# First chunk: q of all heads over its h blocks, k and v beside the h of the next chunks, weights from ScalarE's queue

## The chip, the cores and the metric

The kernel runs on one core of one Trainium2 chip. The metric is the device time of one execution in microseconds; the number compared is the median of several runs. The engines of the core are TensorE (PE; its weight loads are PEld), VectorE (DVE), ScalarE (ACT), GpSimd (POOL) and SyncE (SP), which issues most of the DMAs.

## The reference, cut to what matters

One layer over 2048 tokens of width 1024, in float32:

```
mod = silu(c) @ W_ada + b_ada                  # shift, scale, gate
h = rms_norm(x, norm_g) * (1 + scale) + shift
u = h @ W_in                                   # GLU input, gate_a, q, k, v, gate_b, m_a, m_b
q, k = head_rms_norm(q, q_gain), head_rms_norm(k, k_gain)    # 8 heads of 64
y_a = swish(layer_norm(conv31(glu))) * silu(gate_a) @ W_conv_out
o = stick_breaking_attention(q, k, v)
y_b = (o * silu(gate_b)) @ W_sb_out
x = x + gate * ((sigmoid(m_a) * y_a + sigmoid(m_b) * y_b) @ W_out)
```

## The kernel before, in words

Every matrix product is made of three fp32r products: each operand is split into a high part (a cast) and a low part (operand minus high part), and hi·hi, hi·lo and lo·hi are added in PSUM (`mm3`, `nat_mm`). The tokens are in four chunks of 512, worked from the last to the first (`ORDER`); h of a chunk is held transposed, as eight blocks `kc` of 128 features by 512 tokens, each with a high and a low tile.

**Weights.** `split_into` loads a piece of 128 x 1024 in two halves through two buffers `wl` (SP's queue), casts the half on ScalarE (L109) and subtracts it on GpSimd (L110). A group of q, k or v (256 columns, four heads) is two pieces. Groups 0 and 1 are q, 2 and 3 k, 4 and 5 v.

**The first chunk (pool `hx`).** x tiles are loaded, squared on ScalarE and scaled by the reciprocal root of the mean square (`xn_pair`): three Newton steps, for the first two tiles on VectorE, for the other two on GpSimd. Then a loop over the eight h blocks: two columns of W_ada are loaded and reduced against silu(c) on VectorE (`mod_col`, L225), the one-column scale a_s and shift b_s are made on VectorE (L408, L410), four transposes of x on TensorE give the block, ScalarE makes hf = a_s * x + b_s and its cast hhi, GpSimd the low part hlo (VectorE in the last block). TensorE adds the block's part of q of heads 0 to 3 (group 0), in two PSUM tiles; q of heads 4 to 7 (group 1) is a second loop over the blocks.

**The next chunks.** `h_half` makes h of two x tiles at a time for the chunks ORDER[1], ORDER[2] and, in pool `hz` once `hx` is closed, ORDER[3]: ScalarE hf, VectorE the cast hhi (L366), GpSimd or VectorE hlo (L367). `qk_group` normalises q or k per head: small squares on ScalarE (L272), `head_norm` on VectorE (the root, and qn, L287), `transposed` (four transposes, qhi on ScalarE, qlo on VectorE, L307, one buffer each, four stores to DRAM on SP's queue). For the first chunk's q its squares and `head_norm` run in this part; its transposes run later, through pool `cvp`.

**The rest of the first stage.** With q group 0 of the other chunks done, the stage goes over glu, gate, q, k and v groups in a written order, with matmuls kept in program order on TensorE (`pin`). Each tile ends in a `tick`, which emits RATE taps of the depthwise convolution on VectorE (L485) from a list. PSUM has five buffers `pd`. Here k's two groups and v's first run over all four chunks, v's second (`v_group`) in the next stage, beside the LayerNorm, whose generator `ln` takes a step per tile. Then come the attention and the output stage.

A scheduler orders the instructions of each engine by priority, in the order of the program unless told otherwise; each engine then issues in that fixed order.

Of the kernel before, what the change touches and what calls it, by code (L numbers as in the profile page):

```python
# [8 lines left out]
F32 = mybir.dt.float32  # L9
# [9 lines left out]
P = 128  # L19
# [13 lines left out]
NXT = 7  # L33
NWA = 4
RATE = 2.6
# [15 lines left out]
def trunk_kernel(  # L51
# [29 lines left out]
    def rsqrt(pool, v, n, tag, pool_eng=False, keep=lambda i: i):  # L81
# [3 lines left out]
        keep((nc.gpsimd if pool_eng else nc.vector).tensor_scalar(  # L85
            out=y.bitcast(I32), in0=v.bitcast(I32), scalar1=-0.5, scalar2=MAGIC,
            op0=ALU.mult, op1=ALU.add))
        for _ in range(3):
            if pool_eng:
                nc.gpsimd.tensor_tensor(out=t, in0=y, in1=y, op=ALU.mult)  # L90
                nc.gpsimd.tensor_tensor(out=t, in0=t, in1=v, op=ALU.mult)
                nc.gpsimd.tensor_scalar(out=t, in0=t, scalar1=-0.5, scalar2=1.5,
                                        op0=ALU.mult, op1=ALU.add)
                nc.gpsimd.tensor_tensor(out=y, in0=t, in1=y, op=ALU.mult)
            else:
                keep(nc.vector.scalar_tensor_tensor(out=t, in0=y, scalar=-0.5, in1=y,
                                                    op0=ALU.mult, op1=ALU.mult))
                keep(nc.vector.tensor_tensor(out=t, in0=t, in1=v, op=ALU.mult))
                keep(nc.vector.scalar_tensor_tensor(out=y, in0=t, scalar=1.5, in1=y,
                                                    op0=ALU.add, op1=ALU.mult))  # L100
# [12 lines left out]
    def load_piece(pool, src):  # L113
        hi = pool.tile([P, 1024], F32R, tag="whi", name="whi")
        lo = pool.tile([P, 1024], F32R, tag="wlo", name="wlo")
        split_into(src, hi, lo)
        return hi, lo
# [64 lines left out]
    with ExitStack() as s1:  # L182
# [39 lines left out]
        def mod_col(j, ca, wa):  # L222

            nc.sync.dma_start(wa, w_ada[j])
            nc.vector.scalar_tensor_tensor(out=wa, in0=wa, scalar=1.0, in1=ca,  # L225
                                           op0=ALU.mult, op1=ALU.mult,
                                           accum_out=mod[:, j:j + 1])
# [29 lines left out]
        def qk_group(grp, isk, chunks=ORDER, w2=None, ps0=None):  # L257

            w2 = w2 or ps0 or [piece(w_qkv[grp, i]) for i in range(2)]
            h4 = (grp % 2) * 4  # L260
            dst = kst_d if isk else qst_d
            for b in chunks:
                ssq = sm.tile([P, 4, 4], F32, tag="ssq", name="ssq")
                qn = qp.tile([P, 4, 4, HD], F32, tag="qn", name="qn", bufs=2)
                pss = []
                for half in range(2):
                    ps = ps0[half] if ps0 else nat_tile(pd, w2, b, half)
# [25 lines left out]
        def transposed(qn, pr, dst, h4, b, isk):  # L293
# [5 lines left out]
            hi = cvp.tile([P, CH], F32R, tag="qhi", name="qhi", bufs=1)  # L299
            lo = cvp.tile([P, CH], F32R, tag="qlo", name="qlo", bufs=1)  # L300
# [23 lines left out]


# [3 lines left out]
        def xn_pair(tb0, pool, bufs, pool_eng=False):  # L329
            ss = sm.tile([P, 2], F32, tag="ss", name="ss")  # L330
# [7 lines left out]
            nc.vector.tensor_scalar(out=ss, in0=ss, scalar1=1.0 / D, scalar2=EPS,  # L338
                                    op0=ALU.mult, op1=ALU.add)
            r = rsqrt(sm, ss, 2, "nx", pool_eng)  # L340
            for i in range(2):
                nc.vector.tensor_scalar(out=xs[i], in0=xs[i], scalar1=r[:, i:i + 1],
                                        scalar2=None, op0=ALU.mult)
# [25 lines left out]
        def h_half(g, o, pool, bufs, on_dve):  # L369
            xs = xn_pair(4 * g + o, pool, bufs)  # L370
# [5 lines left out]
        with tc.tile_pool(name="hx", reuse_waits="tile", bufs=1) as hx:  # L376
            g0 = ORDER[0]
            w2_q1 = [(hx.tile([P, D], F32R, name=f"w1h{i}"), hx.tile([P, D], F32R, name=f"w1l{i}"))
                     for i in range(2)]
# [5 lines left out]
            xs = xn_pair(4 * g0, hx, NXT)  # L385
            for o in range(0, D, CH):
# [5 lines left out]
            xs += xn_pair(4 * g0 + 2, hx, NXT, True)  # L392
            ba = load_const(b_ada, 24, "ba")
            ng = load_const(norm_g, KC, "ng")
            ba1 = sm.tile([P, KC], F32, name="ba1", bufs=1)
            nc.vector.tensor_scalar(out=ba1, in0=ba[:, KC:2 * KC], scalar1=1.0, scalar2=None,
                                    op0=ALU.add)
            w2_q0 = []
            qk_ps = [[pd.tile([P, 2, 256], F32, tag="pd", name="pd") for _ in range(2)]
                     for _ in range(2)]  # L400
            for kc in range(KC):
                for j in (8 + kc, kc):
                    mod_col(j, ca, hx.tile([P, D], F32, tag="wa", name="wa", bufs=NWA))
                if kc < 2:
                    w2_q0.append(load_piece(wpa, w_qkv[0, kc]))
                elif kc in (4, 5):
                    split_into(w_qkv[1, kc - 4], *w2_q1[kc - 4])
                nc.vector.tensor_tensor(out=b_s[:, kc:kc + 1], in0=mod[:, kc:kc + 1],  # L408
                                        in1=ba[:, kc:kc + 1], op=ALU.add)
                nc.vector.scalar_tensor_tensor(out=a_s[:, kc:kc + 1], in0=mod[:, 8 + kc:9 + kc],  # L410
                                               scalar=ba1[:, kc:kc + 1], in1=ng[:, kc:kc + 1],
                                               op0=ALU.add, op1=ALU.mult)
                modulate(x_block(xs, kc), hx.tile([P, CH], F32, tag="hf", name="hf", bufs=6),
                         g0, 0, kc, (1, 1),
                         nc.gpsimd if kc < KC - 1 else nc.vector)
                for half in range(2):
                    for i in range(2):
                        nat_mm(qk_ps[0][half], w2_q0, g0, half, i, kc,
                               kc == 0 and i == 0, kc == KC - 1 and i == 1)
            for kc in range(KC):  # L420
                for half in range(2):
                    for i in range(2):
                        nat_mm(qk_ps[1][half], w2_q1, g0, half, i, kc,
                               kc == 0 and i == 0, kc == KC - 1 and i == 1)
            for o in (0, 2):
                h_half(ORDER[1], o, hx, NXT, ())
            qk_group(0, False, ORDER[:1], ps0=qk_ps[0])
            for o in (0, 2):
                h_half(ORDER[2], o, hx, NXT, (0, 4))
            qk_group(1, False, ORDER[:1], ps0=qk_ps[1])  # L430
# [3 lines left out]
        with tc.tile_pool(name="hz", reuse_waits="tile", bufs=1) as hz:  # L434
# [6 lines left out]
            gain = load_const(q_gain, 1, "gain")  # L441
            gk = load_const(k_gain, 1, "gk")
            nc.vector.tensor_tensor(out=gain, in0=gain, in1=gk, op=ALU.mult)


        with tc.tile_pool(name="cvp", reuse_waits="tile", bufs=2, side="right") as cvp:
# [101 lines left out]
            def v_block(grp):  # L548
                w2 = [piece(w_qkv[grp, i]) for i in range(2)]
                h4 = (grp % 2) * 4  # L550
                for b in ORDER:
# [19 lines left out]
            qk_group(2, True)  # L571
            v_block(4)
            glu(3)
            qk_group(3, True)
# [10 lines left out]
        with ExitStack() as sl:  # L585
# [110 lines left out]
            def v_group(grp):  # L696
                w2 = [piece(w_qkv[grp, i]) for i in range(2)]
                h4 = (grp % 2) * 4
                for b in ORDER:
# [397 lines left out]
```

## Time and profile before

| | us |
|---|---|
| median of 3 runs | 1903.24 (1902.55 to 1905.62) |
| profiled execution | 1899.99 |
| its span | 1898.2 |
| TensorE busy in it | 1805.2 (95%) |
| VectorE, ScalarE, GpSimd busy | 1230.8, 807.6, 693.8 |

The rows further down are of the one profiled execution. A busy TensorE is not TensorE at its peak: a matmul of the same size takes longer at the lower of its clocks, and matmuls overlap, so the distance between two starts tells the rate. "Idle before" names what an engine waited for.

### The profile page before, as it was taken

How to read it: one execution, taken by the hardware profiler on the slowest of the kernel's cores; microseconds unless marked ns; L12 is line 12 of the kernel's file. 1: busy time of each engine (PE TensorE's matmuls, PEld its weight loads, DVE VectorE, ACT ScalarE, POOL GpSimd, SP SyncE). 2: the span in 40 equal slices, each digit the busy share in tenths (PEclk: the TensorE clock that was granted, in tenths of full speed). 3: DMA queues.
4: the chain of work that ended last, by engine and by line, in shares of the span. 5: the costliest groups of instructions: out<-in, count | busy, mean ns of one | idle time of the engine just before them, and what ended most of it. 6: DMA issues, size and time to landing. Idle time of an engine off the chain costs nothing.

```text
span 1898.2 us, 27437 instructions
## 1 busy us (share of the span) xinstructions
PE 1805.2 (95%) x9612; PEld 1522.1 (80%) x9612; DVE 1230.8 (65%) x1755; ACT 807.6 (43%) x1988; POOL 693.8 (37%) x931
## 2 busy tenths in 40 slices
PE   5889999999999989999999999999999899999999
PEld 4777898999998888878877777777778677888887
DVE  6873679777777645347777777777777895333341
ACT  4662213132131122247766777767777763010100
POOL 6441102111111133446666666666666741010100
PEclk9899999999999999999999999999999999999999
DMA  7336104044042443342322222232323347353532
GB/s 247 133 93 187 57 21 145 23 122 124 23 128 91 155 151 132 124 137 79 97 81 79 84 84 90 70 95 68 102 66 91 114 149 219 107 160 101 161 94 78
DMA packets 115293, 206.91 MB, mean 109 GB/s; under 512 B 15185, under 2 KB 27473, under 8 KB 115154
## 3 DMA queue, kind: packets, MB, share of 16 engines
q1 hardware_dynamic: 115154, 205.14, 34.8%
q8 instruction: 76, 1.25, 0.3%
q14 instruction: 63, 0.52, 0.1%
HBM read 133.78 MB, written 71.30 MB: 108 GB/s over the span
## 4 chain that ended last, share of the span: by engine, by line
PE 69%; DVE 11%; POOL 6%; issue 6%; DMA 4%; ACT 3%; SPq 0%; DVEq 0%; ACTq 0%; POOLq 0%
PE pd L122 38%; PE po L122 9%; PE p L122 7%; PE av L122 5%; PE pT L127 5%; PE z L122 4%; POOL w L817 3%; DVE sc L810 2%; POOL wlo L110 1%; DVE hhi L366 1%; DMA gt<-ga 1%; DMA wl<-in_w_out_dram 1%; ACT z L806 1%; DVE tlo L844 1%; PE pt L127 1%
## 5 line engine op out<-in xcount | busy, mean ns | idle before, releaser
L817 POOL TENSOR_TENSOR w<-w,sc 128x512 f32<-128x512 f32 (+1 forms) x320 | 361.8, 1131 | 251.7 <-DVE sc L810 178.8
L122 PE MATMUL pd<-hhi,whi 128*128 128x512 f32 x1024 | 411.8, 402 | 0.0
L122 PE MATMUL pd<-hhi,wlo 128*128 128x512 f32 x1024 | 402.1, 393 | 0.0
L122 PE MATMUL pd<-hlo,whi 128*128 128x512 f32 x1024 | 401.6, 392 | 0.0
L810 DVE TENSOR_TENSOR_SCAN sc<-z,sc,w 128x512 f32<-128x512 f32 x192 | 244.8, 1279 | 91.9 <-ACT z L806 84.5
L110 POOL TENSOR_TENSOR wlo<-wl,whi 128x512 fp32r<-128x512 f32 x92 | 134.9, 1477 | 462.0 <-ACT whi L109 461.6
L122 PEld LDWEIGHTS pd<-hhi,wlo 128*128 128x128 f32 x1024 | 192.9, 188 | 41.9
L805 ACT ACTIVATE w<-z 128x512 f32<-128x512 f32 (+1 forms) x320 | 172.3, 538 | 127.4 <-PE z L122 102.8
L122 PE MATMUL pd<-whi,hhi 128*128 128x256 f32 x736 | 216.1, 294 | 6.9 <-DVE qn L287 6.9
L122 PE MATMUL pd<-whi,hlo 128*128 128x256 f32 x736 | 213.6, 292 | 8.9 <-POOL hlo L367 8.6
L122 PEld LDWEIGHTS pd<-hhi,whi 128*128 128x128 f32 x1024 | 194.8, 190 | 33.7
L122 PEld LDWEIGHTS pd<-hlo,whi 128*128 128x128 f32 x1024 | 193.7, 189 | 34.3
L122 PE MATMUL pd<-wlo,hhi 128*128 128x256 f32 x736 | 213.6, 291 | 0.2 <-POOL wlo L110 0.2
L844 DVE TENSOR_TENSOR tlo<-pT,thi 128x512 fp32r<-128x512 f32 (+1 forms) x320 | 183.9, 597 | 34.7 <-ACT thi L843 32.3
L122 PE MATMUL z<-kt,q 128*128 128x512 f32 (+2 forms) x640 | 192.4, 381 | 6.7 <-DVE sc L810 4.0
L843 ACT CAST thi<-pT 128x512 fp32r<-128x512 f32 (+1 forms) x320 | 165.3, 527 | 61.0 <-PE pT L127 57.5
L127 PE MATMUL pT<-ident,w 128*128 128x128 f32 x1088 | 172.2, 273 | 10.5 <-POOL w L817 10.2
L127 PEld LDWEIGHTS pT<-ident,w 128*128 128x128 f32 x1088 | 136.7, 140 | 46.2 <-POOL w L817 15.3
L806 ACT ACTIVATE z<-z 128x512 f32<-128x512 f32 (+1 forms) x320 | 171.8, 537 | 0.0
L122 PEld LDWEIGHTS pd<-whi,hlo 128*128 128x128 f32 x736 | 144.5, 197 | 12.0 <-POOL hlo L367 11.7
L122 PEld LDWEIGHTS pd<-whi,hhi 128*128 128x128 f32 x736 | 146.0, 198 | 7.9 <-DVE qn L287 7.3
L122 PEld LDWEIGHTS pd<-wlo,hhi 128*128 128x128 f32 x736 | 145.9, 198 | 0.7 <-POOL wlo L110 0.4
(274 smaller groups left out, 2984.3 us busy)
## 6 DMA issues: line engine op xcount, KB each, us to landing
wl<-in_w_in_dram SPq DMA_DIRECT2D x64, 256.0 KB, 2.9
wa<-in_w_ada_dram SPq DMA_DIRECT2D x24, 512.0 KB, 5.7
xt<-in_x_n_dram SPq DMA_DIRECT2D x16, 512.0 KB, 5.9
vst<-st SPq DMA_DIRECT2D x64, 128.0 KB, 1.9
kt<-kst SPq DMA_DIRECT2D x32, 256.0 KB, 2.8
vt<-vst SPq DMA_DIRECT2D x32, 256.0 KB, 2.8
q<-qst SPq DMA_DIRECT2D x32, 256.0 KB, 2.9
q<-qst SPq DMA_DIRECT2D x64, 128.0 KB, 3.1
```

The source lines that it names most:

```text
L110: (lo_eng or nc.gpsimd).tensor_tensor(out=lo[:, s], in0=wl, in1=f(hi[:, s]), op=ALU.subtract)
L122: i = nc.tensor.matmul(*a, **k)
L127: i = nc.tensor.transpose(*a)
L366: nc.vector.tensor_copy(hi, hf)
L805: nc.scalar.activation(out=w[:, lo:], in_=z[:, lo:], func=AF.Sigmoid, scale=HD ** -0.5)
L806: nc.scalar.activation(out=z[:, lo:], in_=z[:, lo:], func=AF.Sigmoid, scale=-HD ** -0.5)
L810: nc.vector.tensor_tensor_scan(out=s[:, 1:], data0=z, data1=w, initial=s[:, 0:1], op0=ALU.mult, op1=ALU.bypass)
L817: nc.gpsimd.tensor_tensor(out=w[:, lo:], in0=w[:, lo:], in1=s[:, lo:CH], op=ALU.mult)
L843: nc.scalar.copy(out=thi[:, :n], in_=pT[:, :n])
L844: nc.vector.tensor_tensor(out=tlo[:, :n], in0=pT[:, :n], in1=f(thi[:, :n]), op=ALU.subtract)
```

## The change

The loop over the h blocks takes q of all eight heads (groups 0 and 1) instead of four. Its weights are loaded on ScalarE's queue; their low parts and h's low parts are made on VectorE; a_s and b_s are made on ScalarE. The four x tiles of the first chunk are squared together and get one root; two of the four are scaled on ScalarE; the first two W_ada columns, the root and the scalings stand in a fixed order on VectorE. Then k and v of the first chunk follow, a group at a time, beside the h halves of ORDER[1] and ORDER[2]: `norm_at_once` squares a whole tile on ScalarE, reduces it on VectorE, normalises and transposes at once, with buffers in `hx`. The weights of these groups take over the buffers of the W_ada columns (tag `wa`) and of q's second group (tag `w1`); they come on SP's queue, with the low parts on GpSimd, for group 4 on VectorE. Groups 2 to 5 then leave the first chunk out where they stood, and load their weights again there. NXT is 6 instead of 7, RATE 2.9 instead of 2.6.

```
-NXT = 7
+NXT = 6
-RATE = 2.6
+RATE = 2.9
-    def split_into(src, hi, lo, lo_eng=None):
+    def split_into(src, hi, lo, lo_eng=None, queue=None):
-            nc.sync.dma_start(wl, src[:, s])
+            (queue or nc.sync).dma_start(wl, src[:, s])
...
+        def norm_at_once(pss, grp, b, pool):
+            ssq = sm.tile([P, 4, 4], F32, tag="ssq", name="ssq")
+            qn = qp.tile([P, 4, 4, HD], F32, tag="qn", name="qn", bufs=2)
+            for half in range(2):
+                sq = pool.tile([P, CH], F32, tag="sqv", name="sqv", bufs=1)
+                nc.scalar.activation(out=sq, in_=pss[half].rearrange("p t c -> p (t c)"),
+                                     func=AF.Square)
+                nc.vector.tensor_reduce(
+                    out=ssq[:, 2 * half:2 * half + 2].rearrange("p t h -> p (t h)"),
+                    in_=sq.rearrange("p (n d) -> p n d", d=HD), axis=AX.X, op=ALU.add)
+            head_norm(pss, ssq, qn)
+            for pr in range(2):
+                transposed(qn, pr, kst_d if grp >= 2 else qst_d, (grp % 2) * 4, b, grp >= 2, pool)
...
+        def x_squares(tb0, n, pool, bufs):
...
+        def x_scaled(xs, ss, pool, order=lambda i: i, act=False):
+            n = len(xs)
+            order(nc.vector.tensor_scalar(out=ss, in0=ss, scalar1=1.0 / D, scalar2=EPS,
+                                          op0=ALU.mult, op1=ALU.add))
+            r = rsqrt(pool, ss, n, f"nx{n}", order)
+            for i in range(n):
+                if act and i % 2:
+                    nc.scalar.mul(xs[i], xs[i], r[:, i:i + 1])
+                else:
+                    order(nc.vector.tensor_scalar(out=xs[i], in0=xs[i], scalar1=r[:, i:i + 1],
+                                                  scalar2=None, op0=ALU.mult))
...
+            def hx_piece(src, tag, lo_eng=None, queue=None):
+                hi = hx.tile([P, D], F32R, tag=tag, name="whx", bufs=4)
+                lo = hx.tile([P, D], F32R, tag=tag, name="wlx", bufs=4)
+                split_into(src, hi, lo, lo_eng, queue)
+                return hi, lo
...
             for kc in range(KC):
...
+                if kc in (0, 2):
+                    i = kc // 2
+                    w2_q0.append(load_piece(wpa, w_qkv[0, i], nc.vector, nc.scalar))
+                    w2_q1.append(hx_piece(w_qkv[1, i], "w1", nc.vector, nc.scalar))
+                col = slice(kc, kc + 1)
+                nc.scalar.activation(out=a_s[:, col], in_=mod[:, 8 + kc:9 + kc],
+                                     func=AF.Identity, scale=ng[:, col], bias=ba1[:, col])
+                nc.scalar.activation(out=b_s[:, col], in_=mod[:, col], func=AF.Identity,
+                                     bias=ba[:, col])
                 modulate(x_block(xs, kc), hx.tile([P, CH], F32, tag="hf", name="hf", bufs=6),
-                         g0, 0, kc, (1, 1),
-                         nc.gpsimd if kc < KC - 1 else nc.vector)
+                         g0, 0, kc, (1, 1), nc.vector)
+                for ps2, w2 in zip(qk_ps, (w2_q0, w2_q1)):
+                    for half in range(2):
+                        for i in range(2):
+                            nat_mm(ps2[half], w2, g0, half, i, kc,
+                                   kc == 0 and i == 0, kc == KC - 1 and i == 1)
+            def first(grp, tag, lo_eng=None):
+                w2 = [hx_piece(w_qkv[grp, i], tag, lo_eng) for i in range(2)]
+                return [nat_tile(pd, w2, g0, half) for half in range(2)]
+
+            norm_at_once(qk_ps[0], 0, g0, hx)
+            k0 = first(2, "wa")
+            h_half(ORDER[1], 0, hx, NXT, ())
+            norm_at_once(qk_ps[1], 1, g0, hx)
+            k1 = first(3, "w1")
+            h_half(ORDER[1], 2, hx, NXT, ())
+            norm_at_once(k0, 2, g0, hx)
+            for grp, tag in ((4, "wa"), (5, "w1")):
+                ps2 = first(grp, tag, nc.vector if grp == 4 else None)
                 for half in range(2):
-                    for i in range(2):
-                        nat_mm(qk_ps[0][half], w2_q0, g0, half, i, kc,
-                               kc == 0 and i == 0, kc == KC - 1 and i == 1)
...
+                    v_store(ps2[half], qp.tile([P, D], F32, tag="qn", name="st", bufs=2),
+                            (grp % 2) * 4, g0, half)
+                h_half(ORDER[2], 2 * (grp - 4), hx, NXT, (0, 4))
+                if grp == 4:
+                    norm_at_once(k1, 3, g0, hx)
...
-            qk_group(2, True)
+            qk_group(2, True, ORDER[1:])
...
-            qk_group(3, True)
+            qk_group(3, True, ORDER[1:])
```

In `v_block` and `v_group`, `for b in ORDER` becomes `for b in ORDER[1:]`.

## Rows read from the trace of the kernel before

**Rows 1.** Busy times by stage: engine us (instructions), granted clock, DMA share, GB/s.

```profile
20.00:58.00 38.00, 28.27 (x189) 26.36 (x188) 30.49 (x47) 15.85 (x26) 25.86 (x13) 0.96 0.82 287
58.00:126.00 68.00, 55.56 (x373) 50.07 (x371) 61.00 (x175) 48.05 (x199) 31.28 (x42) 0.90 0.20 64
170.00:620.00 450.00, 449.27 (x2703) 402.33 (x2702) 337.17 (x416) 104.18 (x456) 64.94 (x44) 1.00 0.29 87
```

**Rows 2.** Timeline of TensorE: start us, us, engine, line, operation, tiles.

```profile
24.98 0.41 PE L122 MATMUL pd<-whi,hhi 128*128 128x256 f32 x1
25.19 0.41 PE L122 MATMUL pd<-wlo,hhi 128*128 128x256 f32 x1
...
60.98 0.28 PE L122 MATMUL pd<-w1l,hhi 128*128 128x256 f32 x1
61.10 0.28 PE L122 MATMUL pd<-w1h,hlo 128*128 128x256 f32 x1
...
103.06 0.56 PE L122 MATMUL pd<-whi,hhi 128*128 128x256 f32 x1 [3.04 <-DVE qn L287]
```

**Rows 3.** Chain that ended last up to 220 us: start us, us, what.

```profile
125.16 0.33 DVE hlo L367
...
138.95 5.47 PE pd L122 x24
144.41 0.44 PE pt L127 x4
144.85 5.48 PE pd L122 x24
```

**Rows 4.** Groups of VectorE, 0 to 126 us: count | busy us, mean ns | idle.

```profile
L366 DVE CAST hhi<-hf 128x256 fp32r<-128x256 f32 x48 | 23.4, 531 | 3.7 <-ACT hf L359 3.7
L225 DVE SCALAR_TENSOR_TENSOR wa<-wa,ca 128x1024 f32<-128x1024 f32 x16 | 20.4, 1272 | 4.3 <-DMA wa<-in_w_ada_dram 4.3
L342 DVE TENSOR_SCALAR xt<-xt,nxy 128x1024 f32<-128x1024 f32 x16 | 16.0, 1024 | 3.6 <-POOL nxy L94 3.4
L408 DVE TENSOR_TENSOR b_s<-mod,ba 128x1 f32<-128x1 f32 x8 | 7.0, 870 | 0.2
L410 DVE SCALAR_TENSOR_TENSOR a_s<-mod,ba,ng 128x1 f32<-128x1 f32 x8 | 5.3, 659 | 0.2
...
L287 DVE TENSOR_TENSOR qn<-pd,qry 128x512 f32<-128x512 f32 x6 | 4.0, 683 | 0.1
```

**Rows 5.** Timeline of VectorE in the loop over the h blocks.

```profile
11.51 1.22 DVE L225 SCALAR_TENSOR_TENSOR wa<-wa,ca 128x1024 f32<-128x1024 f32 x1
...
20.61 0.21 DVE L410 SCALAR_TENSOR_TENSOR a_s<-mod,ba,ng 128x1 f32<-128x1 f32 x1
...
24.48 1.21 DVE L225 SCALAR_TENSOR_TENSOR wa<-wa,ca 128x1024 f32<-128x1024 f32 x1
...
25.74 1.11 DVE L410 SCALAR_TENSOR_TENSOR a_s<-mod,ba,ng 128x1 f32<-128x1 f32 x1
...
57.08 0.69 DVE L367 TENSOR_TENSOR hlo<-hf,hhi 128x512 fp32r<-128x512 f32 x1 [2.47 <-ACT hhi L364]
```

**Rows 6.** Waits of SP's queue up to 200 us: total us, times, longest us.

```profile
SPq L334 <- DVE xt L342: 27.5, 2, 21.0
...
SPq L108 <- POOL wlo L110: 15.9, 11, 5.1
```

**Rows 7.** Waits of all engines up to 200 us: total us, times, longest us.

```profile
ACT qhi L306 <- DMA qst<-qhi: 7.8, 4, 3.1
```

**Rows 8.** Group of GpSimd, 0 to 126 us.

```profile
L110 POOL TENSOR_TENSOR wlo<-wl,whi 128x512 fp32r<-128x512 f32 x4 | 7.5, 1905 | 0.0
```

**Rows 9.** Timeline of VectorE: first and last of nine low parts of q.

```profile
126.09 0.68 DVE L307 TENSOR_TENSOR qlo<-pt,qhi 128x512 fp32r<-128x512 f32 x1
...
165.50 0.69 DVE L307 TENSOR_TENSOR qlo<-pt,qhi 128x512 fp32r<-128x512 f32 x1 [0.82 <-DMA qst<-qlo]
```

**Rows 10.** Group of VectorE, 170 to 600 us: a tap.

```profile
L485 DVE SCALAR_TENSOR_TENSOR ca<-u,wdw,ca 128x1025 f32<-128x1025 f32 x54 | 76.7, 1421 | 0.0
```

More of the change, by code (lines that the diff above doesn't have):

```diff
@@ L78, in dram, with rsqrt @@
         return dp.tile(shape, dt, name=name, tag=name)
-    def rsqrt(pool, v, n, tag, pool_eng=False, keep=lambda i: i):
+    def rsqrt(pool, v, n, tag, keep=lambda i: i):
         y = pool.tile([P, n], F32, tag=tag + "y", name=tag + "y")
         t = pool.tile([P, n], F32, tag=tag + "t", name=tag + "t")
-        keep((nc.gpsimd if pool_eng else nc.vector).tensor_scalar(
+        keep(nc.vector.tensor_scalar(
             out=y.bitcast(I32), in0=v.bitcast(I32), scalar1=-0.5, scalar2=MAGIC,
@@ L88, in rsqrt @@
         for _ in range(3):
[L89 to L100, printed above, removed]
+            keep(nc.vector.scalar_tensor_tensor(out=t, in0=y, scalar=-0.5, in1=y,
+                                                op0=ALU.mult, op1=ALU.mult))
+            keep(nc.vector.tensor_tensor(out=t, in0=t, in1=v, op=ALU.mult))
+            keep(nc.vector.scalar_tensor_tensor(out=y, in0=t, scalar=1.5, in1=y,
+                                                op0=ALU.add, op1=ALU.mult))
         return y
-    def split_into(src, hi, lo, lo_eng=None):
+    def split_into(src, hi, lo, lo_eng=None, queue=None):
         for o in range(0, 1024, CH):
@@ L111, in split_into, with load_piece @@
                                                 op=ALU.subtract)
-    def load_piece(pool, src):
+    def load_piece(pool, src, lo_eng=None, queue=None):
         hi = pool.tile([P, 1024], F32R, tag="whi", name="whi")
         lo = pool.tile([P, 1024], F32R, tag="wlo", name="wlo")
-        split_into(src, hi, lo)
+        split_into(src, hi, lo, lo_eng, queue)
         return hi, lo
@@ L224, in mod_col @@
             nc.sync.dma_start(wa, w_ada[j])
-            nc.vector.scalar_tensor_tensor(out=wa, in0=wa, scalar=1.0, in1=ca,
-                                           op0=ALU.mult, op1=ALU.mult,
-                                           accum_out=mod[:, j:j + 1])
+            return nc.vector.scalar_tensor_tensor(out=wa, in0=wa, scalar=1.0, in1=ca,
+                                                  op0=ALU.mult, op1=ALU.mult,
+                                                  accum_out=mod[:, j:j + 1])
         todo = []
@@ L255, in pump, with qk_group @@
                     todo.pop(0)()
-        def qk_group(grp, isk, chunks=ORDER, w2=None, ps0=None):
-            w2 = w2 or ps0 or [piece(w_qkv[grp, i]) for i in range(2)]
+        def qk_group(grp, isk, chunks, w2=None):
+            w2 = w2 or [piece(w_qkv[grp, i]) for i in range(2)]
             h4 = (grp % 2) * 4
@@ L266, in qk_group @@
                 for half in range(2):
-                    ps = ps0[half] if ps0 else nat_tile(pd, w2, b, half)
+                    ps = nat_tile(pd, w2, b, half)
                     pss.append(ps)
@@ L291, in head_norm, with transposed @@
                     op=ALU.mult))
-        def transposed(qn, pr, dst, h4, b, isk):
+        def transposed(qn, pr, dst, h4, b, isk, pool=None):
             ps = pt.tile([P, CH], F32, tag="pt", name="pt")
@@ L298, in transposed @@
                     qn[:, t, 2 * pr:2 * pr + 2, :].rearrange("p h d -> p (h d)"), ident)
-            hi = cvp.tile([P, CH], F32R, tag="qhi", name="qhi", bufs=1)
-            lo = cvp.tile([P, CH], F32R, tag="qlo", name="qlo", bufs=1)
+            hi = (pool or cvp).tile([P, CH], F32R, tag="qhi", name="qhi", bufs=1)
+            lo = (pool or cvp).tile([P, CH], F32R, tag="qlo", name="qlo", bufs=1)
             if isk:
@@ L323, in v_store @@
                 nc.sync.dma_start(vst_d[h4 + i][b][:, 2 * half:2 * half + 2, :], s2[:, i])
+        def norm_at_once(pss, grp, b, pool):
[11 more added lines that the diff above has]
+                transposed(qn, pr, kst_d if grp >= 2 else qst_d, (grp % 2) * 4, b, grp >= 2, pool)
         a_s = sm.tile([P, KC], F32, name="a_s", bufs=1)
         b_s = sm.tile([P, KC], F32, name="b_s", bufs=1)
-        def xn_pair(tb0, pool, bufs, pool_eng=False):
-            ss = sm.tile([P, 2], F32, tag="ss", name="ss")
+        def x_squares(tb0, n, pool, bufs):
+            ss = pool.tile([P, n], F32, tag=f"ss{n}", name="ss")
             xs = []
-            for i in range(2):
+            for i in range(n):
                 xt = pool.tile([P, D], F32, tag="xt", name="xt", bufs=bufs)
@@ L337, in xn_pair @@
                 xs.append(xt)
[L338 to L343, printed above, removed]
+            return xs, ss, pool
+        def x_scaled(xs, ss, pool, order=lambda i: i, act=False):
[3 more added lines that the diff above has]
+            r = rsqrt(pool, ss, n, f"nx{n}", order)
+            for i in range(n):
+                if act and i % 2:
[3 more added lines that the diff above has]
+                                                  scalar2=None, op0=ALU.mult))
             return xs
@@ L369, in h_half @@
         def h_half(g, o, pool, bufs, on_dve):
-            xs = xn_pair(4 * g + o, pool, bufs)
+            xs = x_scaled(*x_squares(4 * g + o, 2, pool, bufs))
             for kc in range(KC):
@@ L377, in trunk_kernel @@
             g0 = ORDER[0]
-            w2_q1 = [(hx.tile([P, D], F32R, name=f"w1h{i}"), hx.tile([P, D], F32R, name=f"w1l{i}"))
-                     for i in range(2)]
+            def hx_piece(src, tag, lo_eng=None, queue=None):
+                hi = hx.tile([P, D], F32R, tag=tag, name="whx", bufs=4)
+                lo = hx.tile([P, D], F32R, tag=tag, name="wlx", bufs=4)
+                split_into(src, hi, lo, lo_eng, queue)
+                return hi, lo
             crow = hx.tile([P, D], F32, tag="wa", name="crow", bufs=NWA)[0:1]
@@ L384, in trunk_kernel @@
             ca = hx.tile([P, D], F32, name="ca", bufs=1)
-            xs = xn_pair(4 * g0, hx, NXT)
+            xs, ss, _ = x_squares(4 * g0, 4, hx, NXT)
             for o in range(0, D, CH):
@@ L391, in trunk_kernel @@
                 nc.vector.tensor_tensor(out=ca[:, s], in0=ps, in1=ca[:, s], op=ALU.mult)
[L392 to L398, printed above, removed]
+            w2_q0, w2_q1 = [], []
             qk_ps = [[pd.tile([P, 2, 256], F32, tag="pd", name="pd") for _ in range(2)]
@@ L401, in trunk_kernel @@
             for kc in range(KC):
+                first_order = tc.keep_in_program_order if kc == 0 else lambda i: i
                 for j in (8 + kc, kc):
[L403 to L409, printed above, removed]
@@ L410, in trunk_kernel @@
-                nc.vector.scalar_tensor_tensor(out=a_s[:, kc:kc + 1], in0=mod[:, 8 + kc:9 + kc],
-                                               scalar=ba1[:, kc:kc + 1], in1=ng[:, kc:kc + 1],
-                                               op0=ALU.add, op1=ALU.mult)
-                modulate(x_block(xs, kc), hx.tile([P, CH], F32, tag="hf", name="hf", bufs=6),
-                         g0, 0, kc, (1, 1),
-                         nc.gpsimd if kc < KC - 1 else nc.vector)
-                for half in range(2):
-                    for i in range(2):
-                        nat_mm(qk_ps[0][half], w2_q0, g0, half, i, kc,
-                               kc == 0 and i == 0, kc == KC - 1 and i == 1)
@@ L420, in trunk_kernel @@
[L420 to L430, printed above, removed]
+                    first_order(
+                        mod_col(j, ca, hx.tile([P, D], F32, tag="wa", name="wa", bufs=NWA)))
@@ new lines, in trunk_kernel @@
+                if kc == 0:
+                    x_scaled(xs, ss, hx, first_order, True)
+                    ba = load_const(b_ada, 24, "ba")
+                    ng = load_const(norm_g, KC, "ng")
+                    ba1 = sm.tile([P, KC], F32, name="ba1", bufs=1)
+                    nc.vector.scalar_tensor_tensor(out=ba1, in0=ba[:, KC:2 * KC], scalar=1.0,
+                                                   in1=ng, op0=ALU.add, op1=ALU.mult)
+                    gain = load_const(q_gain, 1, "gain")
+                    gk = load_const(k_gain, 1, "gk")
+                    nc.vector.tensor_tensor(out=gain, in0=gain, in1=gk, op=ALU.mult)
@@ L550, in v_block @@
                 h4 = (grp % 2) * 4
-                for b in ORDER:
+                for b in ORDER[1:]:
                     for half in range(2):
@@ L698, in v_group @@
                 h4 = (grp % 2) * 4
-                for b in ORDER:
+                for b in ORDER[1:]:
                     for half in range(2):
```

3 lines of the change are left out of this document (removed).

## The prediction

> **What bounds the kernel now.** I read the busy times by stage first [rows 1]: from 170 to 620 us TensorE is busy 449.27 of 450 us, so that stretch is TensorE's own length and what leaves it is worth its full TensorE time. From 58 to 126 us it is VectorE that is full (61.00 of 68) while TensorE is not (55.56, part of it slow). TensorE's real rate shows in its timeline [rows 2]: two 256-column matmuls start 0.21 us apart at 25 us and 0.12 us apart at 61 us, that is 1.2 and 2.4 GHz; at 103 us it waits 3.04 us for VectorE's normalised q and restarts at half clock. The chain [rows 3] shows what sets the early time: it runs through VectorE's h work to the last low part at 125.16 us, and from the first 512-column tile of glu at 138.95 us it is TensorE's, tile after tile. So I reckon to one milestone, the start of that first glu tile: 138.95 us before. Behind it the kernel is TensorE-bound.
>
> **What leaves the TensorE-bound part.** k and v of the first chunk are 4 groups of 2 tiles of 48 matmuls, at 0.12 us [rows 2] 5.76 us a tile, 46.1 us, and 16 transposes for k at 0.11 us (four in 0.44, [rows 3]), 1.8 us. Two of the tiles (v's second group) leave the LayerNorm stage, where TensorE idles a little; I take 0.7 us off. Together 47.2 us. The change gains this, less whatever it delays the milestone.
>
> **The loop over the h blocks.** Removed from VectorE: the 16 one-column operations for a_s and b_s (5.3 + 7.0 us) [rows 4]; they are 0.21 us alone and 1.1 us when GpSimd works beside them [rows 5]. ScalarE takes them over; it was busy 15.85 of 38 us [rows 1]. Removed from GpSimd: all low parts in the loop. VectorE then has 16 w_ada products at 1.27 (20.4), two x scalings at 1.02 (2.0; the other two go to ScalarE), ten small root operations at 0.2 (2.0; one root for four tiles saves the second, which GpSimd did one after another), 8 h low parts at 0.69 (5.5) and 8 weight low parts at the same size (5.5) [rows 4, 5]: 35.4 us. Before, the first w_ada product ran at 11.5 us [rows 5]; from 11 us on this gives 46.5 us for the last h low part, against 57.77 [rows 5]: 11.3 us earlier. q of heads 4 to 7 now runs inside the loop, so TensorE ends q some 3 us later, at 49.7, against 61.2 before [rows 2].
>
> The loop must not wait for data: 4 x tiles, 16 w_ada columns and 4 weight pieces are 24 x 0.52 MB = 12.6 MB. From 20 to 58 us the DMA engines moved 287 GB/s in 0.82 of their time [rows 1], 350 if never idle: 36 us, or 44 at the 287. I take the VectorE sum, and keep 5 us for the slow end. Moving weights to ScalarE's queue takes SP past its waits for weight buffers (15.9 us in 11 up to 200 us [rows 6]); ScalarE gets 8 issues, and a wait wherever a buffer is still held, with h's casts queued behind it. The Trainium skill (DMA: Bandwidth & Descriptors, Issuing engines are not separate DMA queues) says that a second issuing engine saves only issue time. By that rule the 287 GB/s stands, the last w_ada column lands at 45 us and its block's low part ends at 48.5, and the time would be 1883.
>
> **From the loop to the end of h.** In 58 to 126 us VectorE makes the h of three chunks; its last low part ends at 125.5 [rows 3]. It now starts 11.3 us earlier and gets more to do before that point:
> k's two normalisations: 11 small operations (2.2), two qn (0.68 each), two low parts (0.69 each) and two reductions of 512 columns. The trace has no such reduction; its bounds are two casts of 256 columns (1.06) and two qn (1.37) [rows 4]; I take 0.69 as nearest to one pass of 512. Each norm 6.3 us, two 12.6. For q, whose low parts and stores ran after 126 us so far: 4 reductions and 4 low parts, 5.5. v: 4 stores' low parts and the 4 weight low parts that go to VectorE, 5.5. Together 23.6 us.
>
> GpSimd gets 12 more weight low parts (k of both groups, v's second) at 1.9 us, 22.9 us [rows 8], beside VectorE. Bounds: nothing if VectorE is never held, 22.9 if each holds it throughout. Small operations were held 0.9 us [rows 5], but a w_ada product beside GpSimd took its usual 1.21; about one hit of 0.5 for each is 6 us, which I take.
>
> x of the last chunk can load only when the h stage's buffers are closed, and the second of k's and v's weights must wait for the first's buffers. VectorE was idle 7 of 68 us there [rows 1]; the same share over 30 more is 3 us. The bounds are 0 and 10.
>
> TensorE in this stretch gets 8 tiles more (46.1 + 1.8) beside three q tiles' pairs (34.6), 96 x transposes and 40 of q (15): 97.5 us between 49.7 and the milestone. Both engines are then nearly full, and each wait of TensorE costs it a restart at half clock (2.2 us for 24 matmuls, rows 2's spacings); I add 3 us (0 to 8).
>
> Milestone: 138.95 - 11.3 + 23.6 + 6 + 3 + 3 = 163.3, that is 24.3 later. TensorE's own floor is 49.7 + 97.5 = 147.2, below it.
>
> **Costed at nothing.** 16 more weight loads of 256 KB (4.2 MB): DMA is 20% busy in that stage [rows 1]. Their 16 casts, about 10 us at the 0.6 us of a pass over 512 columns: ScalarE has 20 us free there, and the squares of whole tiles save it small operations. If that cover fails, it is in the 10 us above. The taps: 92 ticks at 2.6 become 86 at 2.9, 249 against 239, for the same work. A tap is 1.4 us [rows 10], a glu or gate tile 5.48 [rows 3], so 2.9 taps and an eviction of about 0.7 fill 4.8 of it; in k and q groups VectorE falls behind by some 2 us per chunk (5.8 taps and 5.1 of norm against 11.5), now in three chunks, 6 us, which the five PSUM tiles of 5.5 us cover. Uncovered it would be 4 x 6 = 24 us. VectorE's load from 170 to 620 goes from 337 of 450 [rows 1] to about 326 of 414. The weights of k and v are loaded twice; the later loads are as hidden as now. LayerNorm gets two steps less and conv ends as early in its ticks: nothing, 5 us either way.
>
> **Sum.** 47.2 - 24.3 = 22.9, say 22 us. The profiled execution took 1899.99 us (span 1898.2); it becomes 1878. The median of the runs, 1903.24, lies 3.25 above it, so 1881. The best ends (no contention, idle or restart; 12 us) give a milestone at 151 and 1868; the worst (5 + 17 + 7 + 5 = 34 more) make it 197 and 1914, not all together likely.
>
> **The rivals.**
> Forecast, VectorE and TensorE share the stage nearly full: 0.65, 1868 to 1895.
> The order on the engines keeps k and v from running beside h (they come behind it, TensorE idles as now): the loop's 11.3 us alone remain, and 1892. For it: engines issue in one order, and q's pair waits were seen at 103 us. Against: q tiles did run between x transposes. 0.10.
> TensorE stays at 1.2 GHz through the loop. 28 operations a block at 0.213 are 6.0 us, 8 of them 48, from 20 us on: 68 instead of 49.7, 18 lost, 1899. For it: the spacing of 0.21 at 25 us; against: the loop now has twice the matmuls, and with half it had doubled by 61 us. 0.06.
> SP's queue is blocked: x loads stand behind weight loads that wait for GpSimd (5.1 us at longest [rows 6]; and one of 21 us behind x buffers). Four of the six x pairs late by 5 us: 20, and 1901, no change. 0.08.
> The other side: q and k pass through one pair of transposed buffers, and ScalarE, which also makes h, waits in order for the store of the tile before. Nine such tiles ran from 126.09 to 165.50 us, 4.9 us apart [rows 9]. If all 8 in the new stage hold h that long, 39 us come in place of the 12 for contention, idle and restarts: milestone 190, 51 later, 4 us slower, 1907. It decides from 4.4 us a tile, and each us more a tile is 8 more. Against: ScalarE's measured waits for these stores are 7.8 us in 4, 3.1 at longest [rows 7], and h need not stand behind them. With the tap rate uncovered it would be worse. 0.11.
>
> **Chances and range.** A measurement tells 0.2%, 3.8 us, from no change: under 1899.4 is faster. Forecast and late order give 0.75, the low clock half of its 0.06, of the queue case 0.03: faster 0.81. Same: 0.08. Slower: 0.11. The range 1864 to 1900 takes the forecast with its tail, the late order and the low clock; it leaves out the slow side beyond and the best end's excess.
>
> **What would show it.** Right: w_ada products on VectorE without one-column operations between; the last h low part of the loop near 46.5 us; matmuls of k and v between x transposes; the first glu tile at 155 to 172; from there to the end some 47 us less than the 1759 before. Wrong: GpSimd low parts followed by VectorE idle, ScalarE waiting for stores, x loads late on SP, 0.21 us spacing to the loop's end, TensorE waits for VectorE from 170 to 620, or a stage after the milestone that doesn't shrink.

## The result, and the profile after

The changed kernel takes 1877.08 us in the median of 4 runs (1875.96 to 1879.42); the kernel before took 1904.43 in the runs beside it. The ratio is 0.9858, 95% interval 0.9841 to 0.9876: 27 us faster. The profiled execution took 1879.42 us with a span of 1877.7, 20.5 us less than the span before. The forecast was 1881, with 22 us to gain. The sum came out; how it comes about is another matter.

The busy times by stage of the kernel after, with the columns of [rows 1]:

```profile
20.00:58.00 38.00, 32.19 (x247) 30.84 (x248) 30.16 (x55) 24.92 (x47) 5.14 (x4) 1.00 0.80 276
58.00:126.00 68.00, 58.48 (x463) 56.49 (x462) 54.77 (x147) 35.44 (x71) 27.92 (x31) 0.95 0.57 161
170.00:590.00 420.00, 420.00 (x2441) 372.23 (x2440) 329.67 (x398) 101.81 (x409) 74.19 (x48) 1.00 0.31 94
```

TensorE does more in both early stages (32.19 against 28.27, 58.48 against 55.56). VectorE, which I expected to stay full from 58 to 126 us, is less busy than before: 54.77 against 61.00. The chain of the kernel after:

```profile
163.87 5.75 PE pd L115 x48
...
170.05 5.46 PE pd L115 x24
```

The row of 48 matmuls is a 256-column tile, the row of 24 the first 512-column one. That one, my milestone, is at 170.05 us and not at 163.3. The loss there is made good behind it. To compare all kernels I take one mark that each trace has, the start of the first 512-column matmul of glu in TensorE's timeline (138.70 us before, 0.25 ahead of the chain's row in [rows 3]), and the rest of the span behind it. Mark and rest are of one profiled execution each; the medians of the kernel before, beside which the ratios are taken, lie between 1901.77 and 1904.62 us:

| kernel | first glu tile | rest of the span | median | ratio to before (95%) |
|---|---|---|---|---|
| before | 138.70 | 1759.5 | 1901.77 to 1904.62 | 1 |
| e9: before, RATE 2.9 | 138.49 | 1753.7 | 1893.81 | 0.9956 (0.9941 to 0.9972) |
| e1: loop alone, RATE 2.6 | 125.11 | 1755.8 | 1883.53 | 0.9909 (0.9895 to 0.9923) |
| e10: loop alone, RATE 2.9 | 124.95 | 1749.9 | 1877.99 | 0.9872 (0.9855 to 0.9888) |
| e2: after, RATE 2.6 | 168.41 | 1729.9 | 1901.95 | 0.9999 (0.9989 to 1.001) |
| after | 169.81 | 1707.9 | 1877.08 | 0.9858 (0.9841 to 0.9876) |

The steps before, e1, e10, after add one part at a time. The loop moves the mark 13.6 us forward and takes 3.7 off the rest; RATE takes 5.9 off the rest; k and v beside h put the mark back by 44.9 and take 42.0 off the rest. So the loop gives 17.3 us, RATE 6.1 and the moved k and v minus 2.9. Runs of one kernel differ by 3 to 10 us, and by the medians k and v give 0.9, so the last term can't be told from nothing. The parts don't add in any order either: at the old rate moving k and v (from e1 to e2) makes the span 17.4 us longer. "The loop" here is also the normalisation of q at once, the single root and NXT = 6, which no run takes apart.

### The profile page after: what moved, and what is told of

Same layout as the page of the kernel before. It is cut to its first block, busy times and chain, and to the rows that moved or that the text cites. A ratio compares the mean times of both kernels' runs of the same rounds, so it can differ in the third digit from the quotient of the medians.

```text
span 1877.7 us, 27355 instructions
## 1 busy us (share of the span) xinstructions
PE 1795.9 (96%) x9612; PEld 1517.5 (81%) x9612; DVE 1241.0 (66%) x1763; ACT 814.7 (43%) x1903; POOL 680.3 (36%) x915
## 4 chain that ended last, share of the span: by engine, by line
PE 71%; DVE 6%; POOL 5%; DMA 4%; issue 3%; ACT 3%; SPq 0%; DVEq 0%; ACTq 0%; POOLq 0%
PE pd L115 39%; PE po L115 9%; PE p L115 7%; PE av L115 5%; PE pT L120 5%; PE z L115 5%; POOL w L850 3%; DVE sc L843 2%; DMA gt<-ga 1%; DMA wl<-in_w_out_dram 1%; DVE tlo L877 1%; POOL wlo L103 1%; ACT z L839 1%; PE pt L120 1%; ACT w L838 1%
## 5 line engine op out<-in xcount | busy, mean ns | idle before, releaser
L115 PE MATMUL pd<-whi,hhi 128*128 128x256 f32 x608 | 173.8, 286 | 3.4 <-DVE sg L577 1.7
L115 PE MATMUL pd<-whi,hlo 128*128 128x256 f32 x608 | 172.9, 286 | 0.7 <-DVE hlo L382 0.7
L115 PE MATMUL pd<-wlo,hhi 128*128 128x256 f32 x608 | 172.4, 284 | 0.0
L847 DVE TENSOR_TENSOR_SCAN sc<-z,tri 128x512 f32<-128x512 f32 (+3 forms) x128 | 104.4, 819 | 53.2 <-ACT z L839 41.6
L115 PE MATMUL av<-tlo,vt 128*128 128x512 f32 (+1 forms) x320 | 122.6, 383 | 12.7 <-DVE tlo L877 9.5
L115 PEld LDWEIGHTS z<-kt,q 128*128 128x128 f32 x640 | 109.7, 190 | 26.4 <-DVE sc L843 6.6
```

Source lines behind the costliest of these rows:

```text
L115: i = nc.tensor.matmul(*a, **k)
L847: nc.vector.tensor_tensor_scan(out=s[:, lo + 1:], data0=z[:, lo:], data1=tri[:, :CH - lo], initial=1.0, op0=ALU.mult, op1=ALU.max)
```

## The experiments

**The loop alone (e1).** The new loop, the normalisation of q at once, but no k and v in the first stage, and the old tap rate.

```
-RATE = 2.9
+RATE = 2.6
-            k0 = first(2, "wa")
-            k1 = first(3, "w1")
...
+            for o in (0, 2):
+                h_half(ORDER[2], o, hx, NXT, (0, 4))
...
-            qk_group(2, True, ORDER[1:])
+            qk_group(2, True, ORDER)
```

> The changed loop alone (q of all heads in it, ScalarE's queue, low parts on VectorE, one root), with q normalised at once, while k and v of the first chunk stay where they were and RATE is 2.6. My theory: the moved k and v give most of the gain, so this one loses what they gave; the loop's end moved from 57.77 to 52.57 us, 5 us, so 3 to 9 us faster than before (1895 to 1901), and the first glu tile some 5 us before 138.95 us. Rival (the loop is what gives it): within 5 us of the changed kernel, 1877 to 1882.

0.9909 (0.9895 to 0.9923), and the first glu tile at 125.11 us, 13.6 earlier. I had expected 3 to 9 us; the rival was nearer. The loop itself ends only 5 us earlier than before; its last low part in VectorE's timeline of e1:

```profile
51.90 0.68 DVE L382 TENSOR_TENSOR hlo<-hf,hhi 128x512 fp32r<-128x512 f32 x1
```

That is 52.6 against 57.8 [rows 5]. The rest comes at the other end: from the last low part of h to the first glu tile it was 13.2 us before and is 4.7 in e1. q of both head groups is now normalised beside h, so no transposes of q stand between h and glu. TensorE's waits from 126 to 170 us in the kernel before (total us, times, longest) show it; the first of the three falls behind the mark, the other two ahead of it, and e10 has none in that stretch:

```profile
PE pt L127 <- DVE qn L287: 3.8, 1, 3.8
PE pt L127 <- DVE qlo L307: 2.6, 1, 2.6
PE pt L127 <- DVE qry L85: 2.2, 1, 2.2
```

**The old tap rate (e2).** The changed kernel with `RATE = 2.6`, nothing else.

> RATE back to 2.6, all else as changed. My theory: the taps are covered either way, within 2 us of 1877, with the LayerNorm stage's TensorE waits at most 3 us longer because conv ends later. Rival (the saving after the milestone that exceeded my 47.2 us comes from the rate): 4 to 8 us slower than the changed kernel.

My theory, within 2 us of the changed kernel, failed. The whole gain is gone: 0.9999 (0.9989 to 1.001). The mark stands where it stood; the rest of the span is 22 us longer. TensorE's waits from 590 to 700 us in e2, and then VectorE's last pass over the conv's sums:

```profile
PE mub L115 <- ACT hl L668: 20.0, 1, 20.0
```

```profile
648.28 1.22 DVE L528 TENSOR_TENSOR cc<-cc,ca 128x1024 f32<-128x1024 f32 x1
```

The LayerNorm's first matmul needs the finished conv. With 86 ticks of 2.6 taps the conv ends at 649.5 us and TensorE stands 20.0 us. The kernel's text shows how: the list that the ticks draw from holds 213 entries, and what a tick may draw while the list is empty is lost. Counted through, the kernel before has 1 entry left after its last tick, e2 has 17, and the changed kernel is done one tick before the end. The 17, passes like the one above, are some 21 us of VectorE behind the last tick. In the changed kernel the same pass is over by 618.43 us, and no such wait is left:

```profile
617.21 1.22 DVE L528 TENSOR_TENSOR cc<-cc,ca 128x1024 f32<-128x1024 f32 x1
```

**The new tap rate on the kernel before (e9), and on the loop alone (e10).** The first is the kernel before with `RATE = 2.9`, the second is e1 with it.

> The kernel before with RATE 2.9 and nothing else. Undoing the rate alone cost the changed kernel its whole gain. My theory now: 2.9 only makes up for the six ticks that the moved k and v take out of the first stage; with all 92 ticks the rate has little to give, the 3.5 us wait of the mean's matmul for conv: 0 to 5 us faster than before. Rival (the rate itself is the gain): over 12 us faster.

> The changed loop alone (k and v stay) with RATE 2.9. My theory: the loop gives most of the gain, and TensorE had only some 3 us more of idle that k and v could fill, so with the rate this one comes within 4 us of the changed kernel, 1878 to 1882. Rival (k and v moved are worth what the ratios suggest, 9 us): 1884 or more.

RATE alone gives 0.9956 (0.9941 to 0.9972), some 8 us, more than my theory's 0 to 5. The kernel before already paid a little for a late conv: VectorE's last pass over its sums, and TensorE's first matmul of the LayerNorm with the wait ahead of it:

```profile
636.24 2.20 DVE L495 TENSOR_TENSOR cc<-cc,ca 128x1024 f32<-128x1024 f32 x1
```

```profile
656.19 1.52 PE L122 MATMUL mub<-hl,onesr 128*128 128x512 f32 x2 [3.54 <-ACT hl L635]
```

In e9 the same two matmuls start at 650.68 without a wait and take 0.62 us, not 1.52; the granted clock from 655 to 660 us is 1.00 there and 0.66 before. The loop with the new rate, and with k and v where they always were, gives 0.9872 (0.9855 to 0.9888): all that the whole change gives. Moving k and v, the largest term of my sum, is worth nothing as the change does it.

**Weights from SP's queue (e3).** `queue` dropped from the loop's `load_piece` and `hx_piece`.

```
-                    w2_q0.append(load_piece(wpa, w_qkv[0, i], nc.vector, nc.scalar))
+                    w2_q0.append(load_piece(wpa, w_qkv[0, i], nc.vector))
```

> The loop's weights on SP's queue again, low parts still on VectorE. My theory: the loop's loads are mixed in another order and w_ada columns wait behind weight buffers; between 2 us faster (x scaled earlier, since ScalarE has no cast that waits 4.5 us for its piece ahead of x) and 5 us slower; the first hf block near 21 us instead of 24.8. Rival (the queue is what made the loop faster): the loop ends 5 to 10 us later, 1882 to 1887.

0.9876 (0.9859 to 0.9892), the same time as after. But the loop starts quite otherwise. ScalarE's timeline of the kernel after, and then of e3:

```profile
21.30 0.62 ACT L102 CAST whi<-wl 128x512 fp32r<-128x512 f32 x1 [4.49 <-DMA wl<-in_w_qkv_dram]
21.83 2.19 ACT L355 ACTIVATE xt<-xt,nx4y 128x1024 f32<-128x1024 f32 x2
...
24.80 0.78 ACT L374 ACTIVATE hf<-pt,b_s,a_s 128x512 f32<-128x512 f32 x1 [0.27 <-PE pt L120]
```

```profile
14.64 2.19 ACT L355 ACTIVATE xt<-xt,nx4y 128x1024 f32<-128x1024 f32 x2 [0.97 <-DVE nx4y L92]
...
17.73 0.78 ACT L374 ACTIVATE hf<-pt,b_s,a_s 128x512 f32<-128x512 f32 x1 [0.40 <-PE pt L120]
```

In the changed kernel the scaling of x stands on ScalarE behind a cast that waits 4.49 us for its weights, and the first h comes 7 us later than in e3. Yet the loop of e3 ends only 1.7 us earlier (VectorE's last low part there is at 49.74 for 1.09 us). So VectorE's sum does not set the pace: from 10 to 50 us VectorE was busy 29.94 of 40 us after. The last w_ada product starts at 48.20 us after and at 45.96 in e3, each having waited for its DMA, though only 0.28 and 0.23 us. That the transfers pace both is argued; no run with fewer bytes was made. The Trainium skill (DMA: Bandwidth & Descriptors, Issuing engines are not separate DMA queues) says that a second issuing engine saves only issue time. The traces agree: from 20 to 58 us 276 GB/s were moved with the weights on ScalarE's queue, 288 with them on SP's (e3) and 287 before [rows 1].

**The loop's low parts on GpSimd again (e4).** Weights' low parts, and h's but for the last block, as before.

```
-                         g0, 0, kc, (1, 1), nc.vector)
+                         g0, 0, kc, (1, 1), nc.gpsimd if kc < KC - 1 else nc.vector)
```

> Low parts of weights and h in the loop on GpSimd again, as before the change. My theory: 16 low parts of 1.3 to 2.3 us on GpSimd hold VectorE's one-port operations little now that a_s and b_s are on ScalarE, but the chain h low part to TensorE lengthens: loop end 3 to 8 us later and 2 to 7 us slower than the changed kernel. Rival (VectorE is the loop's bound, so taking 11 us of work off it helps): the loop ends earlier and the time falls by 2 to 5 us.

0.9923 (0.9909 to 0.9937): 1886.84 us, 9.8 more than after. The loop's last h low part ends at 56.2 us, 3.7 later, and the first glu tile is at 177.43 us, 7.6 later. Having the loop's low parts on VectorE is a good part of what the loop gives.

**All low parts of the early weights on VectorE (e7), and with SP's queue (e11).** In `first`, every group's low parts:

```
-                w2 = [hx_piece(w_qkv[grp, i], tag, lo_eng) for i in range(2)]
+                w2 = [hx_piece(w_qkv[grp, i], tag, nc.vector) for i in range(2)]
```

> All weight low parts of the first chunk's k and v on VectorE, none on GpSimd. My prediction charged 6 us for 12 of them holding VectorE. If so, 8.3 us more VectorE work less that hold: within 3 us. Theory now (VectorE is idle 13 of 68 us in that stage, and GpSimd's 1.3 to 2.5 us each is longer than VectorE's 0.69): 0 to 4 us faster. Rival (VectorE is the stage's bound, as I predicted): 2 to 8 us slower.

> k and v moved, all their weight low parts on VectorE, and the loop's weights on SP's queue again. Theory (the two edits act in different places: the first glu tile came 6.5 us earlier by the one, 2.9 by the other): 9 us earlier together, the milestone near 160.5 us, 1868 to 1871. Rival (one wait takes the other's place): no better than the low parts alone, 1871 to 1874.

e7 takes 1871.44 us, 0.9838 (0.9818 to 0.9857), e11 1871.08, 0.9827 (0.981 to 0.9844); of one another they can't be told apart, as the rival of e11 had it, and they are the fastest kernels of this study. Their intervals still overlap a little with that of after, but each of their nine runs is below each of its four. More work for the engine that I held to be full makes the kernel faster: the first glu tile is at 163.29 us in e7. Part of the reason is seen where VectorE runs the root of the next x tiles. VectorE's timeline of the kernel after, then GpSimd's:

```profile
54.00 0.16 DVE L91 TENSOR_TENSOR nx2t<-nx2t,ss 128x2 f32<-128x2 f32 x1
54.19 1.24 DVE L92 SCALAR_TENSOR_TENSOR nx2y<-nx2t,nx2y 128x2 f32<-128x2 f32 x1
```

```profile
54.12 1.30 POOL L103 TENSOR_TENSOR wlx<-wl,whx 128x512 fp32r<-128x512 f32 x1 [2.10 <-PE pd L115]
```

An operation on two columns takes 0.16 us, or 1.24 when it meets a weight low part of GpSimd: it ends when that ends (55.43 and 55.42 us). One group of these small operations from 45 to 126 us (count, busy us, mean ns, idle), after and then e7:

```profile
L91 DVE TENSOR_TENSOR nx2t<-nx2t,ss 128x2 f32<-128x2 f32 x12 | 4.0, 337 | 0.2
```

```profile
L91 DVE TENSOR_TENSOR nx2t<-nx2t,ss 128x2 f32<-128x2 f32 x12 | 1.9, 157 | 0.2
```

Its mean falls from 337 to 157 ns; with the other small root operations of that stretch it is 8.0 us less in e7. A low part on VectorE costs 0.69 us of it, on GpSimd up to 1.1 of it each time that it meets one of these. But the 12 more low parts take 8.5 us of VectorE in e7, and its busy time from 45 to 126 us is the same, 64.46 after and 64.53 in e7. So VectorE has no less to do; what shrinks is TensorE's idle time. The stage row (columns of [rows 1]) and TensorE's longest wait in it, after and then e7:

```profile
56.00:163.00 107.00, 94.29 (x746) 91.45 (x746) 84.55 (x229) 58.21 (x164) 42.61 (x51) 0.95 0.46 138
PE pt L120 <- DVE qn L280: 7.1, 2, 5.1
```

```profile
56.00:163.00 107.00, 97.85 (x795) 95.33 (x794) 79.68 (x236) 61.06 (x182) 31.77 (x43) 0.98 0.47 140
PE pt L120 <- DVE qn L280: 4.2, 2, 2.5
```

TensorE is busy 3.6 us more, most of it by a shorter wait for the normalised q and k (qn), and the granted clock is 0.98 instead of 0.95, an estimated 3.2 us of 107. Together that is about what the first glu tile gains (6.5). e7 does two things at once, though: it takes the GpSimd passes off the small operations, and it makes each weight low part shorter (0.69 against 1.3 us). No run separates them.

**The loop alone with SP's queue (e14), only v moved (e13).** e14 is e10 with e3's edit; e13 is e11 with only groups 4 and 5 beside h. "The first run" of the two expectations is e11.

> The changed loop with SP's queue and RATE 2.9, k and v not moved. Theory: 1 to 3 us faster than the same with ScalarE's queue (1878), and 3 to 8 us slower than the first run of this call, which would be what k and v are worth once their low parts are off GpSimd. Rival (moving k and v is worth nothing however it is done): within 2 us of the first run.

> As the first run of this call, but only v of the first chunk is moved; k stays. Theory (TensorE's idle before the milestone is filled by the first few tiles, the rest only changes places): within 3 us of the first run, with the milestone about 24 us earlier than there and the stretch behind it longer by as much. Rival (k's tiles fill idle that v's can't): 4 us or more slower than the first run.

e14: 1880.43 us, 0.9871 (0.985 to 0.9891), first glu tile at 126.28. e11 beside it is 9.3 us faster by the medians, and the two intervals just miss each other (0.985 and 0.9844): its mark is 39.0 us later and the rest 46.5 shorter. So with no weight low part of the early groups on GpSimd the move of k and v does pay, by some 8 us. e13 takes 1875.05 us, 0.9839 (0.9821 to 0.9857), between the two, 4.0 us above e11 but not to be told from it: its mark comes 20.6 us earlier than e11's and the rest is 24.9 longer.

**Order and stores (e12, e8).** e12 is e11 with each `h_half` issued ahead of the weights and tiles of its group; e8 is the changed kernel with the stores of v's first chunk on ScalarE's queue, since on SP's the x loads of the last chunk stand behind them. "The run before" of e12's expectation is e11.

```
-                ps2 = first(grp, tag, nc.vector if grp == 4 else None)
...
+                h_half(ORDER[2], 2 * (grp - 4), hx, NXT, (0, 4))
+                ps2 = first(grp, tag)
```

> The kernel of the run before in this call (low parts on VectorE, SP's queue) with each h half written ahead of the group of k or v beside which it stands. Theory (TensorE's order puts a group's 11.5 us of matmuls ahead of the transposes that VectorE, ScalarE and GpSimd wait for): h ends 3 to 8 us earlier and the time falls by 2 to 6 us. Rival (the groups' weights, or the norms, set the pace): the same within 2 us, or slower since TensorE is left idle first.

> The changed kernel with the first chunk's v stored from ScalarE's queue. The last chunk's x loads stood behind 7 v stores on SP's queue until 127.12 us. Theory (the milestone is paced by those loads): they start 4 to 6 us earlier, the first glu tile 3 to 5 us earlier, 1872 to 1875. Rival (the loads wait for the buffers that v's matmuls free, or TensorE's order holds the h halves back): within 1.5 us of the changed kernel.

e12 takes 1878.01 us, 0.9861 (0.9844 to 0.9877), 7 more than e11, so TensorE does not gain by having h first. e8 is at 0.9872 (0.9855 to 0.9889), as after. SP's queue of the changed kernel has the pattern that I feared, seven issues of v's stores and then the x loads,

```profile
121.43 5.59 SPq L316 DMA_DIRECT2D vst<-st  x7
...
127.12 2.97 SPq L342 DMA_DIRECT2D xt<-in_x_n_dram  x4
```

but with the stores moved away the x loads are issued at 125.39 us, only 1.7 earlier and not the 4 to 6 expected: stores of k stand ahead of them too. So e8 shows that the queue of v's stores costs nothing, and leaves open what earlier x loads would give. Two buffers for the transposed q and k, which would test my slower rival directly, were not tried.

## Why the prediction was right, and where only its sum was

**The milestone** was a good place to cut: from there to 590 us TensorE is busy throughout (420.00 of 420 us from 170 on). But further on it is not TensorE alone that counts, as e2's 20.0 us show.

**What leaves the TensorE-bound part**, 47.2 us: measured 42.0 from e10 to after, 46.5 from e14 to e11. The term is right in size; the 4.5 us between the two are no more than runs of one kernel differ by.

**The loop**, 11.3 us by VectorE's sum: its end moved by 5.2. The step that failed is the choice of the VectorE sum over the transfers. VectorE waits 12.4 us from 10 to 53 us, 6.7 of them for casts of weights and 3.2 for w_ada, and e3, where the first h comes 7 us earlier, ends the loop 1.7 earlier. The price by the transfers, a last low part at 48.5, was nearer to the 52.6 measured. Still the loop gave 17.3 us, for a reason that my sum had only as a cost: it charged 5.5 us of VectorE for q's norm beside h and credited nothing for its absence behind h, where 8.5 us went (13.2 to 4.7).

**From the loop to the end of h**, 35.6 us later: measured 44.9 by the mark, from e10 to after. The contention of 12 GpSimd low parts, taken at 6 us, is 8.0 us of VectorE's small operations by e7, and without it the mark comes 6.5 earlier: the size holds, though VectorE is no less busy then. The rest was 29.6 and measures 38.3 (e10 to e7). It rested on VectorE being full, and this failed: VectorE has 13 of 68 us free. TensorE's path, which I had put below the milestone at 147.2 us, is what the mark is made of. Its row for the stage, in the kernel after:

```profile
55.00:170.00 115.00, 102.29 (x814) 99.45 (x813) 86.37 (x232) 62.51 (x187) 44.51 (x53) 0.96 0.46 136
```

TensorE ends q near 55.4 us instead of 49.7. With the 97.5 us of work of my sum (the trace has 16 transposes fewer, 1.8 us), 12.7 us idle, and 4.6 us lost by a granted clock of 0.96 (an estimate, 0.04 of 115), that makes 170.2; the mark is 169.81. So the term that was too small is the 3 us for TensorE's waits and restarts: it is some 17. The longest waits are for the normalised q and k (7.1 us in 2), x (3.2 in 3) and h (2.0 in 2). Not each wait costs a restart, as I had it: before, the clock stayed at 1.00 from 140 to 150 us, behind the wait of 2.58 us at 138.32. What would shorten these waits, only e7 and e11 show in part: e12 tried one other order and lost, and e8 hardly moved the x loads.

**Costed at nothing.** The taps are the step that failed outright. I compared 249 taps with 239 and left the conv's end where it was, plus or minus 5 us. It ends 20 us earlier than before (618.4 against 638.4), and RATE alone gives 8 us on the kernel before. What counts is not 249 against 239 but how many of the 213 entries are left after the last tick. That my price for lost cover, 24 us, is near what the old rate costs (22 us) is luck: the mechanism is another, not VectorE behind in the k and q groups but the LayerNorm waiting for the conv (20.0 us in e2), and the price counts four such groups where three stand behind the milestone, 18 us. ScalarE's queue and v's stores do cost nothing (e3, e8).

**The rivals.** The late order would have given the loop alone, 1892: k and v did run beside h, and the loop alone gave 1878 to 1883. The low clock did not come: from 20 to 58 us the granted clock was 1.00. The queue case, 1901, and the slower side, 1907, did not come either; whether a second pair of transposed buffers would gain anything is open.

So the time was right because errors cancelled, and that is luck: against the sum's 11.3 for the loop and 11.6 for k and v (47.2 less 35.6), less 1 in rounding, stand 17.3, 6.1 from a term set to zero, and minus 2.9.

## What to carry to other kernels

When the amount of work between two points changes, ask of each thing paced by a count of steps (here taps per tile) when it ends, and which wait that end feeds, before costing it at nothing. Moving TensorE work into an earlier stage that is not TensorE-bound gains only the idle time that it really fills there: price the stage's end after the move, not the work that leaves the later one. Work taken from between two stages is worth its place as well as its length, so credit what it no longer delays.

## What the hardware showed that I had not expected

A VectorE operation on 2 columns with two operands took up to 1.24 us in place of 0.16 whenever it met a GpSimd pass over 128x512, and ended with it, while a pass of 512 columns of VectorE's own is 0.69 us. The Trainium skill (SBUF — State Buffer, Who interferes with whom) says that a VectorE instruction with two inputs in SBUF contends with a GpSimd instruction that reads SBUF, and that the port pair they share is an exclusive lock. The trace agrees: of the small root operations from 50 to 130 us, each that starts within a GpSimd pass ends with it, to 0.1 us. e7, which takes 12 of these passes off GpSimd, is 6 us faster; how much of that is the lock's, no run tells. A reduction of 512 columns on VectorE, which the trace of before did not have, takes about what I took for it: 0.68 us (L326, the first at 57.82 us after) against 0.69.
